# A transformer layer in split fp32: the last output-projection columns by token halves, operand combinations in order of need, and gate2 in 1 KB pieces

## Chip, core and metric

The kernel runs on one core of one Trainium2 chip. The metric is device microseconds of one execution. The median of three runs of the kernel before is 1672.77 us (1672.48 to 1673.21).

## The reference

One layer of a decoder for 1024 tokens of width 1024, all in fp32. What matters here is its end:

```python
mod = c_act @ w_ada[l] + b_ada[l]
shift1, scale1, gate1, shift2, scale2, gate2 = [m[:, None, :] for m in jnp.split(mod, N_MOD, axis=-1)]
...
y = jax.nn.sigmoid(g_a) * y_a + jax.nn.sigmoid(g_b) * y_b
x = layer_norm_affine(ALPHA * x + gate1 * (y @ w_o[l]), ln1_g[l], ln1_b[l])

h2 = layer_norm(x) * (1.0 + scale2) + shift2
u = h2 @ w_up[l]
up = jnp.pad(u, ((0, 0), (CONV_W - 1, 0), (0, 0)))
u = conv_b[l] + sum(conv_w[l, t] * up[:, t:t + S] for t in range(CONV_W))
u_gate, u_val = jnp.split(u, 2, axis=-1)
f = jax.nn.gelu(u_gate, approximate=False) * u_val
x = layer_norm_affine(ALPHA * x + gate2 * (f @ w_down[l]), ln2_g[l], ln2_b[l])
```

`w_o` is 1024 x 1024, `w_up` 1024 x 5632, `w_down` 2816 x 1024, `w_ada` 1024 x 6144.

## The kernel before

**Arithmetic.** Every fp32 operand of TensorE (PE) is split into a high part rounded to fp32r and the rest as a low part, and a product is three matmuls (high by high, high by low, low by high). `split_to()` does it with a cast on ScalarE (ACT, L378) and a subtraction on VectorE (DVE, L379, the tiles ending in `l` or `lo`). The weights come through staging tiles `wst` (four buffers) and `raw` (six).

**Order of the work.** PE's order is written out by hand: `unit()` issues the matmuls of one product, moves a model clock `now` on by a cost, and between them `run_due()` calls whatever `at(delay, ...)` has put into a queue for that moment. The instructions of the other engines follow their place in the program and are set in order from it; every engine, and SyncE (SP), which issues the loads and stores, works off its own list in order.

**Output projection.** `wo_unit(n, t)` computes 256 output columns `n` of token tile `t` (128 tokens): `o_unit()` loads the residual x (tile `th`, later `xt`), runs 24 matmuls into a `pj` bank, and `o_evac()` (L979) adds it to alpha x, giving `y`. The weights are folded with gate1 on their way (L250, cast L252, split L253). Columns 0:256 and 256:512 are done so; the groups of weights are in `g_o`. The last columns, 512:1024, are `o_unit(t, g_o[2], 512, 512, ...)` for the eight token tiles in order, after all 256-column units. At that point the pools of the stage before, with the `th` tiles, are closed, and the pool `hq` takes their place.

**Layer norms.** After each of the last units `ln_a()` takes statistics (L364, L366), gets the reciprocal root `rs` on GpSimd (POOL, L357 and L358), normalises on DVE (L1059, L1060) and stores the row tile; `ln_b()` takes statistics again and writes the second norm on ACT (L1065). `h2_part()` transposes it on PE (L1076), evacuates by ACT (L1081, tiles `xt`, `t3hf`, `t4hf`), and splits: the first 512 tokens on DVE and POOL (L1084, L1085); for the second 512 DVE builds differences.

**Up projection.** It multiplies 2 x 2 blocks of `w_up` and h2 with seven products for eight. The moving operands are the blocks themselves (`h2h`, `h2l`), and the combinations T1 = B12 - B11 (`t3lf` at L1067 first), T2 = B22 - T1 (`t4lf`, then `t2h`/`t2l`), T3 = B22 - B12 (`t3h`/`t3l`) and T4 = B21 - T2 (`t4h`/`t4l`, with L1116). `h2_rest()` writes, after the last part of h2, the splits of T1, then all of T3, then those of B22 and all of T4, each for k = 0 to 3. `product(n)` runs the list `seq`; product 6 uses T2, 7 uses T3, 4 uses T4. Products 4, 6 and 7 share a pair of PSUM banks (`w`); the pair is free again when DVE has added both to the hidden tile `u` (L1244). Weight combinations are summed on POOL (L1179 to L1185), loads are at L1167, the convolution's steps at L1146 (tile `cv`).

**gate2** is a product of a vector and `w_ada`, done on DVE: `ada_part(3, kt)` loads two pieces of 128 x 512 into `wst` buffers (256 KB each, name `aw`), and `ada_acc()` multiplies (L596) or multiplies and adds (L598) them into `gate`. Eight parts follow each other from `ADA3_D = 100` us of the model clock on, every `ADA3_P = 12`; `ada_end(3)` sums over partitions on PE (L615) and adds the bias on DVE (L616).

**The end.** The down projection is accumulated for token tiles in the order `(0, 2, 3, 1)` of each half; `finish()` gates, adds the residual, takes statistics and normalises (L1301 to L1310). For `t == NT - 1` the last step is one DVE operation (L1312), for all others ACT scales (L1314) and POOL adds (L1315).

## Time and profile before

| | |
|---|---|
| median of three runs | 1672.77 us (1672.48 to 1673.21) |
| the profiled execution | 1667.94 us |
| its span, first to last instruction | 1666.2 us |
| mean granted TensorE clock in it | 0.98 |
| busy: PE, DVE, ACT, POOL | 1570.1, 1083.1, 739.0, 509.8 us |
| PE busy from 880 to 980 us | 68.9 of 100 us |

The profiled execution is one run of its own, with its own time; its events are measured from the span's start. "Busy" is the time in which an engine executes an instruction; a wait belongs to the engine's next instruction and is put down to the event that came last (the releaser). The granted clock is given as a share of full speed.

### The profile page before, as it was taken

How to read it: one execution, taken by the hardware profiler on the slowest of the kernel's cores; microseconds unless marked ns; L12 is line 12 of the kernel's file. 1: busy time of each engine (PE TensorE's matmuls, PEld its weight loads, DVE VectorE, ACT ScalarE, POOL GpSimd, SP SyncE). 2: the span in 40 equal slices, each digit the busy share in tenths (PEclk: the TensorE clock that was granted, in tenths of full speed). 3: DMA queues.
4: the chain of work that ended last, by engine and by line, in shares of the span. 5: the costliest groups of instructions: out<-in, count | busy, mean ns of one | idle time of the engine just before them, and what ended most of it. 6: DMA issues, size and time to landing. Idle time of an engine off the chain costs nothing.

```text
span 1666.2 us, 28016 instructions
## 1 busy us (share of the span) xinstructions
PE 1570.1 (94%) x10513; PEld 1389.9 (83%) x10514; DVE 1083.1 (65%) x2092; ACT 739.0 (44%) x1698; POOL 509.8 (31%) x694
## 2 busy tenths in 40 slices
PE   5899999999999999999998768989999999999996
PEld 4899999998998999989996556777788887888885
DVE  7766666675646545535658878777877877437535
ACT  5565555554535544545313624433444444333430
POOL 5523232232633614415316442222332220003103
PEclk9999999999999999999999989999999999999998
DMA  7501000013214032111142322333222215743641
GB/s 248 163 24 36 27 27 27 27 52 116 64 52 127 26 102 89 52 51 29 49 158 95 102 64 76 108 108 104 81 89 82 77 63 197 249 142 115 195 139 51
DMA packets 77769, 153.36 MB, mean 92 GB/s; under 512 B 8753, under 2 KB 11313, under 8 KB 77634
## 3 DMA queue, kind: packets, MB, share of 16 engines
q1 hardware_dynamic: 77634, 151.58, 28.6%
q8 instruction: 82, 1.34, 0.3%
q14 instruction: 53, 0.43, 0.1%
HBM read 131.63 MB, written 19.92 MB: 91 GB/s over the span
## 4 chain that ended last, share of the span: by engine, by line
PE 80%; DVE 9%; DMA 3%; POOL 3%; issue 3%; ACT 2%; SPq 0%; POOLq 0%; ACTq 0%; DVEq 0%
PE pj L334 10%; PE pj L336 10%; PE pj L335 10%; PE w L1292 7%; PE pj L1292 4%; PE m L1292 3%; PE w L1234 3%; PE w L1236 3%; PE w L1235 3%; DMA aw<-in_ada 2%; PE m L712 2%; PE m L1234 2%; PE m L1235 2%; PE m L1236 2%; PE pj L349 2%
## 5 line engine op out<-in xcount | busy, mean ns | idle before, releaser
L334 PE MATMUL pj<-whi,hh 128*128 128x256 f32 (+1 forms) x1296 | 374.0, 289 | 0.1
L336 PE MATMUL pj<-whi,hl 128*128 128x256 f32 (+1 forms) x1296 | 367.7, 284 | 0.0
L335 PE MATMUL pj<-wlo,hh 128*128 128x256 f32 (+1 forms) x1296 | 367.5, 284 | 0.0
L334 PEld LDWEIGHTS pj<-whi,hh 128*128 128x128 f32 x1296 | 248.6, 192 | 0.6 <-issue 0.2
L335 PEld LDWEIGHTS pj<-wlo,hh 128*128 128x128 f32 x1296 | 247.0, 191 | 0.6 <-issue 0.2
L336 PEld LDWEIGHTS pj<-whi,hl 128*128 128x128 f32 x1296 | 246.9, 191 | 0.0
L378 ACT CAST whi<-wst 128x512 fp32r<-128x512 f32 x176 | 107.3, 619 | 152.2 <-PE w L1235 49.2
L379 DVE TENSOR_TENSOR wlo<-wst,whi 128x512 fp32r<-128x512 f32 x176 | 132.2, 762 | 58.7 <-ACT whi L378 58.5
L1146 DVE SCALAR_TENSOR_TENSOR cv<-u,pv_sb,cv 128x1023 f32<-128x1023 f32 x88 | 119.4, 1359 | 12.3 <-ACT cv L1144 12.3
L357 POOL TENSOR_SCALAR rs<-mv 128x1 f32<-128x1 f32 x32 | 15.5, 488 | 319.0 <-DVE mv L1305 249.3
L253 DVE TENSOR_TENSOR wlo<-wst,whi 128x512 fp32r<-128x512 f32 (+1 forms) x108 | 78.5, 744 | 42.1 <-ACT whi L252 41.6
L252 ACT CAST whi<-wst 128x512 fp32r<-128x512 f32 (+1 forms) x116 | 70.5, 620 | 42.7 <-PE pj L336 27.1
L379 DVE TENSOR_TENSOR fl<-wst,fh 128x512 fp32r<-128x512 f32 x41 | 29.0, 708 | 80.6 <-ACT fh L378 80.6
L378 ACT CAST whi<-raw 128x512 fp32r<-128x512 f32 x66 | 40.8, 620 | 90.3 <-PE m L1235 43.3
L691 POOL TENSOR_SCALAR_AFFINE_SELECT pch<-ph 128x512 f16<-128x512 f16 x32 | 20.4, 639 | 195.7 <-ACT ph L686 195.7
L1179 POOL TENSOR_TENSOR raw<-raw 128x512 f32<-128x512 f32 x22 | 33.6, 1528 | 141.2 <-DMA raw<-in_wup 69.1
L1185 POOL TENSOR_TENSOR wst<-wst 128x512 f32<-128x512 f32 x22 | 35.8, 1626 | 127.6 <-issue 88.3
L1234 PE MATMUL pj<-h2h,whi 128*128 128x512 f32 x176 | 70.6, 401 | 1.7 <-ACT u L1241 1.7
L1236 PE MATMUL pj<-h2h,wlo 128*128 128x512 f32 x176 | 69.8, 397 | 1.5 <-DVE wlo L379 1.5
L1235 PE MATMUL pj<-h2l,whi 128*128 128x512 f32 x176 | 69.8, 396 | 0.0
L1234 PE MATMUL m<-h2h,whi 128*128 128x512 f32 x176 | 69.8, 396 | 0.0
L1235 PE MATMUL m<-h2l,whi 128*128 128x512 f32 x176 | 69.2, 393 | 0.0
(441 smaller groups left out, 4469.9 us busy)
## 6 DMA issues: line engine op xcount, KB each, us to landing
wst<-in_wbig SPq DMA_DIRECT2D x112, 256.0 KB, 3.1
aw<-in_ada SPq DMA_DIRECT2D x96, 256.0 KB, 3.2
wst<-in_wdn SPq DMA_DIRECT2D x88, 256.0 KB, 3.1
wst<-in_wup SPq DMA_DIRECT2D x52, 256.0 KB, 2.6
raw<-in_wup SPq DMA_DIRECT2D x44, 256.0 KB, 3.4
fd<-cv SPq DMA_DIRECT2D x22, 512.0 KB, 4.1
wst<-fd SPq DMA_DIRECT2D x44, 256.0 KB, 3.1
y<-in_x SPq DMA_DIRECT2D x8, 512.0 KB, 8.4
```

The source lines that it names most:

```text
L252: act.copy(out=hi, in_=st)
L253: lo_eng.tensor_tensor(out=lo, in0=st, in1=hi.bitcast(F32), op=ALU.subtract)
L334: pe.matmul(acc, lhsT=lh, rhs=wh, start=kt == 0 if start is None else start, stop=False)
L335: pe.matmul(acc, lhsT=lh, rhs=wl, start=False, stop=False)
L336: pe.matmul(acc, lhsT=ll, rhs=wh, start=False, stop=kt == NK - 1 if stop is None else stop)
L378: act.copy(out=hl[0], in_=src)
L379: dve.tensor_tensor(out=hl[1], in0=src, in1=hl[0].bitcast(F32), op=ALU.subtract)
L1146: dve.scalar_tensor_tensor(out=c_[:, lag:S], in0=u[:, 0:S - lag], scalar=wv[:, 2 - lag:3 - lag], in1=c_[:, lag:S], op0=ALU.mult, op1=ALU.add)
L1234: pe.matmul(acc, lhsT=wh[:, kt, :], rhs=bh, start=p not in (2, 3) and kt == 0, stop=False, **go)
L1235: pe.matmul(acc, lhsT=wh[:, kt, :], rhs=bl, start=False, stop=False, **go)
L1236: pe.matmul(acc, lhsT=wl[:, kt, :], rhs=bh, start=False, stop=kt == 3, **go)
L1292: pe.matmul(acc, lhsT=l_[:, ts_], rhs=r_, start=i == 0 and n == 0, stop=i == NFF - 1 and n == 2)
```

## The change

1. The last columns' weights are no longer streamed by `ws`. Eight pieces are loaded to `wst`, multiplied by the gate, and split into the slots of T3 and T4 (`t_slot(3, ...)`, `t_slot(4, ...)`), which are free until the second half of h2.
2. The eight last-columns units and the four units of columns 256:512 of the second token half are one list: the first last-columns unit comes first, then they alternate.
3. `h2_rest()` is gone. `t1_t3(k)` and `b22_t4(k)` are put into the queue one by one, every 2.0 and 2.6 us of the model clock.
4. gate2 is computed by 32 pieces of 128 x 256 (1 KB per partition) and four of one row for the bias, in one buffer of its own (`aw3`), from 70 us of the model clock on, one every 8.5. ACT evacuates the sums of `ada3_end()`.
5. In `finish()` the one-operation DVE path is taken for the last tile worked on in the second half.


```diff
--- before.py
+++ after.py
@@ -34,8 +34,9 @@
 B_FIRST = 3
 B_LAST = (3, 5)
 MOD_PE = 1
-ADA3_D = 100.0
-ADA3_P = 12.0
+ADA3_D = 70.0
+ADA3_P = 8.5
+T3_P, T4_P = 2.0, 2.6
 ADA_D = 5.0
 ADA_E = 8
 LN_D = 5.0
@@ -285,11 +286,14 @@
         g_qk.append(add_group())
         g_ga.append(add_group())
         g_v.append(add_group())
-    g_o = [add_group(fold=(0, slice(0, 256))), add_group(fold=(0, slice(256, 512))),
-           add_group(fold=(0, slice(512, 1024)), shape=(1, 512), n=8)]
+    g_o = [add_group(fold=(0, slice(0, 256))), add_group(fold=(0, slice(256, 512)))]
+    wi_o2 = wi
+
     def kslice(ids, kt):
 
         base = 0
+        if isinstance(ids[0], tuple):
+            return ids[kt]
         for w_ in ids:
             n = ws.items[w_][1][0]
             if kt < base + n:
@@ -1028,7 +1032,7 @@
     yT[1] = new_yT(1)
     for t in range(4):
         at((0.3, 2.0, 4.0, 9.5)[t], 0.87, lambda t=t: y_transpose(4 + t))
-    for n, t in ((1, 0), (1, 1), (0, 4), (1, 2), (0, 5), (1, 3), (0, 6), (1, 4), (0, 7)):
+    for n, t in ((1, 0), (1, 1), (1, 2), (1, 3), (0, 4), (0, 5), (0, 6), (0, 7)):
         wo_unit(n, t)
     assert not queue
     s2ctx.close()
@@ -1044,11 +1048,16 @@
         return hq.tile([P, 512], dtype, name=f"t{m}{hl}" + ("" if dtype == F32R else "f"), tag=f"t{m}{hl}", bufs=4)
 
     g1b, b1b = (hq.tile([P, D], F32, name=n_, tag="t2h", bufs=2) for n_ in ("g1b", "b1b"))
-    for t in range(5, NT):
-        wo_unit(1, t)
-    sp.dma_start(g1b, rows[2])
-    sp.dma_start(b1b, rows[3])
-    ws.get(g_o[2][-1])
+    g_o2 = []
+    for kt in range(NK):
+        st = wp.tile([P, 512], F32, name="wst", tag="wst", bufs=4)
+        sp.dma_start(st, wbig[wi_o2 + kt])
+        if kt == 3:
+            sp.dma_start(g1b, rows[2])
+            sp.dma_start(b1b, rows[3])
+        dve.tensor_tensor(out=st, in0=st, in1=gate[:, 512:1024], op=ALU.mult)
+        g_o2.append(tuple(t_slot(3 + kt // 4, hl, kt % 4) for hl in "hl"))
+        split_to(g_o2[kt], st)
     h2 = [None, None]
 
     def ln_a(t):
@@ -1097,40 +1106,65 @@
             tt_[2][k] = t2h[0][:, k % 2, :], t_slot(2, "l", k)
             split_to(tt_[2][k], t2)
 
-    def h2_rest():
-
-        for k in range(4):
-            split_to([hl[:, :, k, :] for hl in h2[1]], rows4(tmp.pop(("t1", k))))
-        for k in range(4):
-            b12, b22 = tmp.pop(("b", k)), tmp["b", 4 + k]
-            t3 = hq.tile([P, 512], F32, name="xt", tag="raw", bufs=6)
-            sub(t3, b22, b12)
-            tt_[3][k] = [t_slot(3, hl, k) for hl in "hl"]
-            split_to(tt_[3][k], t3)
-        for k in range(4):
-            b22 = rows4(tmp.pop(("b", 4 + k)))
-            split_to([hl[:, :, 4 + k, :] for hl in h2[1]], b22)
-            t4 = hq.tile([P, 512], F32, name="xt", tag="raw", bufs=6)
-            b21 = [hl[:, :, 4 + k, :].bitcast(F32) for hl in h2[0]]
-            sub(rows4(t4), b21[0], rows4(tmp.pop(("t2", k))))
-            dve.tensor_tensor(out=rows4(t4), in0=rows4(t4), in1=b21[1], op=ALU.add)
-            tt_[4][k] = [t_slot(4, hl, k) for hl in "hl"]
-            split_to(tt_[4][k], t4)
+    def t1_t3(k):
+
+        b12, b22 = tmp.pop(("b", k)), tmp["b", 4 + k]
+        t3 = hq.tile([P, 512], F32, name="xt", tag="raw", bufs=6)
+        sub(t3, b22, b12)
+        tt_[3][k] = [t_slot(3, "h", k), None]
+        act.copy(out=tt_[3][k][0], in_=t3)
+        split_to([hl[:, :, k, :] for hl in h2[1]], rows4(tmp.pop(("t1", k))))
+        tt_[3][k][1] = t_slot(3, "l", k)
+        dve.tensor_tensor(out=tt_[3][k][1], in0=t3, in1=tt_[3][k][0].bitcast(F32), op=ALU.subtract)
+
+    def b22_t4(k):
+
+        b22 = rows4(tmp.pop(("b", 4 + k)))
+        split_to([hl[:, :, 4 + k, :] for hl in h2[1]], b22)
+        t4 = hq.tile([P, 512], F32, name="xt", tag="raw", bufs=6)
+        b21 = [hl[:, :, 4 + k, :].bitcast(F32) for hl in h2[0]]
+        sub(rows4(t4), b21[0], rows4(tmp.pop(("t2", k))))
+        dve.tensor_tensor(out=rows4(t4), in0=rows4(t4), in1=b21[1], op=ALU.add)
+        tt_[4][k] = [t_slot(4, hl, k) for hl in "hl"]
+        split_to(tt_[4][k], t4)
 
     def ln_tile(t):
         ln_a(t)
         at(LN_D, 0.0, lambda: ln_b(t))
 
-    for t in range(NT):
-        o_unit(t, g_o[2], 512, 512, lambda: ln_tile(t))
-        if t % 4 == 3:
-            for n in range(NK):
-                kt = n if t == 3 else n // 2 + 4 * (n % 2)
-                at(H2_D + H2_P * n, 0.45, lambda kt=kt, t=t: h2_part(t // 4, kt))
-    at(H2_D + H2_P * NK, 0.0, h2_rest)
-    for kt in range(NK):
-        at(ADA3_D + ADA3_P * kt, 0.0, lambda kt=kt: ada_part(3, kt))
-    at(ADA3_D + ADA3_P * NK + 40.0, 1.7, lambda: ada_end(3))
+    def ada3_part(kt, j):
+
+        cs = slice(256 * j, 256 * j + 256)
+        aw = hq.tile([P, 256], F32, name="aw3")
+        if kt < NK:
+            sp.dma_start(aw, ada2[3 * NK + kt][:, cs])
+            ada_acc(aw, cs, kt)
+        else:
+            sp.dma_start(aw[0:1, :], rows[1][0:1, cs])
+            dve.tensor_tensor(out=gate[0:1, cs], in0=gate[0:1, cs], in1=aw[0:1, :], op=ALU.add)
+
+    def ada3_end(i):
+        cs = slice(512 * i, 512 * i + 512)
+        pt = ps1("m")
+        pe.matmul(pt, lhsT=ones, rhs=gate[:, cs], start=True, stop=True)
+        act.copy(out=gate[:, cs], in_=pt)
+
+    for n, t in ((2, 0), (1, 4), (2, 1), (1, 5), (2, 2), (1, 6), (2, 3), (1, 7), (2, 4), (2, 5), (2, 6), (2, 7)):
+        if n < 2:
+            wo_unit(n, t)
+        else:
+            o_unit(t, g_o2, 512, 512, lambda: ln_tile(t))
+        if n == 2 and t % 4 == 3:
+            for m in range(NK):
+                kt = m if t == 3 else m // 2 + 4 * (m % 2)
+                at(H2_D + H2_P * m, 0.45, lambda kt=kt, t=t: h2_part(t // 4, kt))
+    for k in range(4):
+        at(H2_D + H2_P * NK + T3_P * k, 0.0, lambda k=k: t1_t3(k))
+        at(H2_D + H2_P * NK + T3_P * 4 + T4_P * k, 0.0, lambda k=k: b22_t4(k))
+    for m in range(4 * (NK + 1)):
+        at(ADA3_D + ADA3_P * m, 0.0, lambda m=m: ada3_part(m // 4, m % 4))
+    for i in range(2):
+        at(ADA3_D + ADA3_P * 4 * (NK + 1) + 10.0 * i, 1.4, lambda i=i: ada3_end(i))
 
 
 
@@ -1291,7 +1325,7 @@
         for n, (l_, r_) in enumerate(((fh, wh), (fh, wl), (fl, wh))):
             pe.matmul(acc, lhsT=l_[:, ts_], rhs=r_, start=i == 0 and n == 0, stop=i == NFF - 1 and n == 2)
 
-    def finish(s, tl):
+    def finish(s, tl, last):
         t = 4 * s + tl
         z = xts.pop(t)
         st = sq.tile([P, 2, 6], F32, name="bst")
@@ -1308,7 +1342,7 @@
             cs = slice(512 * hf, 512 * hf + 512)
             zs = z[:, cs]
             dve.scalar_tensor_tensor(out=zs, in0=zs, scalar=mv[:, 0:1], in1=g2b[:, cs], op0=ALU.subtract, op1=ALU.mult)
-            if t == NT - 1:
+            if last:
                 dve.scalar_tensor_tensor(out=zs, in0=zs, scalar=rs, in1=b2b[:, cs], op0=ALU.mult, op1=ALU.add)
             else:
                 act.activation(out=zs, in_=zs, func=AF.Identity, scale=rs)
@@ -1358,7 +1392,7 @@
             for hf in range(2):
                 for i in range(NFF - n_last, NFF):
                     down_mm(s, i, tl, hf)
-            finish(s, tl)
+            finish(s, tl, s == 1 and tl == order[-1])
```

The planned order of three lists shows what moved. First DVE's list at the first last-columns evacuation (`y<-xt,pj 128x512`) and its weight splits. Before:
```order
L253 TENSOR_TENSOR wlo<-wst,whi 128x512
L250 TENSOR_TENSOR wst<-wst,gate 128x512 x3
L979 SCALAR_TENSOR_TENSOR y<-xt,pj 128x256 x2
L253 TENSOR_TENSOR wlo<-wst,whi 128x512 x3
L979 SCALAR_TENSOR_TENSOR y<-xt,pj 128x256
L250 TENSOR_TENSOR wst<-wst,gate 128x512
L253 TENSOR_TENSOR wlo<-wst,whi 128x512
L979 SCALAR_TENSOR_TENSOR y<-xt,pj 128x512
L364 BN_STATS bst<-y 128x6
L366 BN_AGGR mv<-bst 128x2
L1059 SCALAR_TENSOR_TENSOR y<-y,mv,g1b 128x1024
```
After the change:
```order
L983 SCALAR_TENSOR_TENSOR y<-th,pj 128x256 x6
L383 TENSOR_TENSOR t3l<-wst,t3h 128x512 x4
L1058 TENSOR_TENSOR wst<-wst,gate 128x512 x2
L383 TENSOR_TENSOR t4l<-wst,t4h 128x512
L1058 TENSOR_TENSOR wst<-wst,gate 128x512
L383 TENSOR_TENSOR t4l<-wst,t4h 128x512
L1058 TENSOR_TENSOR wst<-wst,gate 128x512
L383 TENSOR_TENSOR t4l<-wst,t4h 128x512 x2
L983 SCALAR_TENSOR_TENSOR y<-xt,pj 128x512
L368 BN_STATS bst<-y 128x6
L370 BN_AGGR mv<-bst 128x2
L1068 SCALAR_TENSOR_TENSOR y<-y,mv,g1b 128x1024
```
The four `t3l` splits and four `t4l` splits of the last weights stand where the stream's `wlo` splits stood; the evacuation of the 512-column unit comes before four of the 256-column ones instead of behind them.

Then DVE's list around the first evacuation of a product into `u`. Before:
```order
L1067 TENSOR_TENSOR xt<-h2h,t4lf 128x512
L379 TENSOR_TENSOR h2l<-t4hf,h2h 128x4x128
L379 TENSOR_TENSOR t4l<-xt,t4h 128x512
L1116 TENSOR_TENSOR xt<-xt,h2l 128x512
L1067 TENSOR_TENSOR xt<-h2h,t4lf 128x512
L379 TENSOR_TENSOR wlo<-raw,whi 128x512
L379 TENSOR_TENSOR t4l<-xt,t4h 128x512
L1116 TENSOR_TENSOR xt<-xt,h2l 128x512
L1244 TENSOR_TENSOR u<-w_13674,u 128x512
L379 TENSOR_TENSOR wlo<-wst,whi 128x512
L379 TENSOR_TENSOR t4l<-xt,t4h 128x512
L1244 TENSOR_TENSOR u<-w_13674,u 128x512
```
After the change:
```order
L383 TENSOR_TENSOR t2l<-t4lf,t2h 128x512
L1118 TENSOR_TENSOR t3l<-xt,t3h 128x512
L383 TENSOR_TENSOR h2l<-t3lf,h2h 128x4x128
L383 TENSOR_TENSOR wlo<-raw,whi 128x512
L1118 TENSOR_TENSOR t3l<-xt,t3h 128x512
L1076 TENSOR_TENSOR xt<-t4hf,t3hf 128x512
L383 TENSOR_TENSOR h2l<-t3lf,h2h 128x4x128
L1278 TENSOR_TENSOR u<-w_13622,u 128x512
L1118 TENSOR_TENSOR t3l<-xt,t3h 128x512
L383 TENSOR_TENSOR wlo<-wst,whi 128x512
L1076 TENSOR_TENSOR xt<-t4hf,t3hf 128x512
L383 TENSOR_TENSOR h2l<-t3lf,h2h 128x4x128
```
The evacuation stood behind all T3 and nearly all T4 work; it now stands ahead of half of the T3 splits and of all T4 work.

Last, SP's list of loads and stores in the part where the last token tiles are normalised. Before:
```order
L987 DMA xt<-in_x 128x512
L1061 DMA x1d<-y 128x1024 x6
L987 DMA xt<-in_x 128x512
L1167 DMA wst<-in_wup 128x512
L1061 DMA x1d<-y 128x1024
L1167 DMA raw<-in_wup 128x512 x2
L1167 DMA wst<-in_wup 128x512 x2
L1167 DMA raw<-in_wup 128x512 x2
L1167 DMA wst<-in_wup 128x512
L1061 DMA x1d<-y 128x1024
```
After the change (`aw_...` are the loads of gate2):
```order
L991 DMA xt<-in_x 128x512
L1070 DMA x1d<-y 128x1024
L1140 DMA aw_14161<-in_ada 128x256
L1140 DMA aw_14230<-in_ada 128x256
L1070 DMA x1d<-y 128x1024
L1140 DMA aw_14301<-in_ada 128x256
L1140 DMA aw_14366<-in_ada 128x256
L1201 DMA wst<-in_wup 128x512 x2
L1070 DMA x1d<-y 128x1024
L1201 DMA wst<-in_wup 128x512 x2
L1140 DMA aw_14426<-in_ada 128x256
L1070 DMA x1d<-y 128x1024
```
The loads of gate2, which came behind this part, now stand between the weight loads and the stores of the normalised rows.

## Rows read from the trace of the kernel before

**Rows 1.** The page, part 1: busy time of each engine, its share, instructions.
```profile
PE 1570.1 (94%) x10513; PEld 1389.9 (83%) x10514; DVE 1083.1 (65%) x2092; ACT 739.0 (44%) x1698; POOL 509.8 (31%) x694
```

**Rows 2.** Busy time by stretches: stretch, length, engines, PEclk (granted clock), DMA share, GB/s.
```profile
880.00:980.00 100.00, 68.92 (x306) 53.64 (x305) 82.13 (x123) 45.56 (x71) 54.13 (x55) 0.90 0.27 87
...
960.00:980.00 20.00, 10.01 (x37) 8.07 (x38) 15.55 (x23) 3.82 (x7) 13.21 (x7) 0.67 0.20 54
```

**Rows 3.** PE's waits, 860 to 1000: who <- for whom: total us, times, longest.
```profile
PE w L1234 <- DVE u L1244: 14.5, 2, 13.7
```

**Rows 4.** DVE's time line: start, us, instruction, [idle before <- releaser].
```profile
863.53 0.69 DVE L979 SCALAR_TENSOR_TENSOR y<-xt,pj 128x512 f32<-128x512 f32 x1 [1.78 <-PE pj L336]
...
934.66 1.78 DVE L1067 TENSOR_TENSOR t3lf<-t3hf,h2h 128x512 f32<-128x512 f32 x1
...
954.80 0.68 DVE L379 TENSOR_TENSOR t2l<-t4lf,t2h 128x512 fp32r<-128x512 f32 x1
...
956.00 1.89 DVE L1067 TENSOR_TENSOR xt<-t4hf,t3hf 128x512 f32<-128x512 f32 x3
...
969.24 0.69 DVE L1244 TENSOR_TENSOR u<-w,u 128x512 f32<-128x512 f32 x1
```

**Rows 5.** PE's waits, 1000 to 1320.
```profile
PE w L1234 <- DVE u L1244: 17.5, 5, 5.9
PE m L615 <- DVE gate L616: 0.8, 1, 0.8
```

**Rows 6.** PE's time line in the gate2 stretch.
```profile
1067.82 0.51 PE L1234 MATMUL w<-t4h,whi 128*128 128x512 f32 x1 [0.77 <-DVE u L1244]
...
1087.83 0.79 PE L1234 MATMUL w<-t3h,whi 128*128 128x512 f32 x1 [5.86 <-DVE u L1244]
...
1092.93 0.40 PE L1234 MATMUL m<-h2h,whi 128*128 128x512 f32 x1
...
1132.40 0.50 PE L1234 MATMUL w<-t3h,whi 128*128 128x512 f32 x1 [3.19 <-DVE u L1244]
...
1175.02 0.50 PE L1234 MATMUL w<-t3h,whi 128*128 128x512 f32 x1 [2.03 <-DVE u L1244]
```

**Rows 7.** DVE's time line at the eighth unit of the projection.
```profile
846.35 0.42 DVE L979 SCALAR_TENSOR_TENSOR y<-th,pj 128x256 f32<-128x256 f32 x1 [2.45 <-PE pj L336]
847.71 2.12 DVE L253 TENSOR_TENSOR wlo<-wst,whi 128x512 fp32r<-128x512 f32 x3 [0.94 <-ACT whi L252]
...
851.29 1.32 DVE L250 TENSOR_TENSOR wst<-wst,gate 128x512 f32<-128x512 f32 x2 [0.52 <-DMA wst<-in_wbig]
```

**Rows 8.** The tile gate, 1000 to 1250: instructions (min/median/max ns), DVE's idle before them.
```profile
L598 DVE SCALAR_TENSOR_TENSOR gate<-aw,csil,gate x14: 740/752/1344, 1068.9 to 1163.5; 128x512 f32<-128x512 f32 x14
...
  DMA aw<-in_ada: 14.9, 12
```

**Rows 9.** DMA issues: count, size, median us to landing (from 810; from 1040).
```profile
th<-in_x SPq DMA_DIRECT2D x10, 128.0 KB, 2.2
...
aw<-in_ada SPq DMA_DIRECT2D x16, 256.0 KB, 3.1
```

**Rows 10.** DVE's time line at the first pair of gate2 pieces.
```profile
1048.60 0.49 DVE L596 TENSOR_SCALAR gate<-aw,csil 128x512 f32<-128x512 f32 x1 [1.06 <-DMA aw<-in_ada]
...
1052.48 0.49 DVE L596 TENSOR_SCALAR gate<-aw,csil 128x512 f32<-128x512 f32 x1 [2.20 <-DMA aw<-in_ada]
```

**Rows 11.** Time lines of DVE, ACT and POOL at the end.
```profile
1653.56 1.41 DVE L1312 SCALAR_TENSOR_TENSOR xr<-xr,rs,b2b 128x512 f32<-128x512 f32 x2
...
1659.77 1.33 ACT L1314 ACTIVATE xr<-xr,rs 128x512 f32<-128x512 f32 x2 [13.12 <-POOL rs L358]
...
1660.56 2.48 POOL L1315 TENSOR_TENSOR xr<-xr,b2b 128x512 f32<-128x512 f32 x2 [0.83 <-ACT xr L1314]
```

**Rows 12.** DVE by line, 862 to 975: busy us, mean ns | idle before.
```profile
L1060 DVE SCALAR_TENSOR_TENSOR y<-y,rs,b1b 128x1024 f32<-128x1024 f32 x8 | 12.3, 1537 | 4.8 <-POOL rs L358 4.6
```

**Rows 13.** Waits of SP's own queue, 840 to 1000.
```profile
SPq L1167 <- DVE wlo L379: 70.7, 18, 27.1
```

## The prediction, made before the changed kernel ran

> **What bounds the kernel now.** I read the page first: TensorE (PE) is busy for 94% of the span [rows 1], so a change pays only where PE stands. The busy time by stretches shows where that is: between 880 and 980 us PE loses 31 of 100 us. In the last 20 of them it works 10.0 us while VectorE (DVE) works 15.6, and the granted clock has fallen to 0.67 of full speed, between its two levels of 1.2 and 2.4 GHz [rows 2]. The table of PE's waits names the largest of these losses: 13.7 us for the DVE evacuation of `u` at L1244 [rows 3]. DVE's own time line shows why. The chain begins at 863.5, when the first last-columns product is evacuated; the first T1 difference (`t3lf`) comes at 934.7, the last low part of T2 at 954.8, and the `u` evacuation for which PE waits only at 969.2, because h2_rest() put nearly all T1, T3, `b22` and T4 work ahead of it [rows 4]. So DVE bounds the stretch 863 to 970, and PE has products ready to run that wait for one 0.6 us evacuation behind 14 us of operands for later products. A second place is the accumulation of gate2 (1045 to 1210): PE waits for `u` there again, at 1067.8, 1087.8, 1132.4 and 1175.0; with one of 5.6 us before it, at 1006, these are the five of the table [rows 5, 6].
>
> A difference of 0.2% (3.3 us) is about what a measurement of this kernel can tell from none.
>
> **The change, term by term.** The sum is made against the profiled execution, 1667.9 us (span 1666.2); the median of the runs shown is 4.8 us above that.
>
> *Start of the last columns.* Four 256-column units move behind the first 512-column one. Units follow each other by 2.85 us, so that product could begin at 846.4, when the eighth unit is evacuated [rows 7], instead of 857.8 (its 24 matmuls at 0.24 us take 5.7, and its evacuation starts at 863.5): 11.4 us earlier. But its weights now lie in `t3`/`t4` slots of a pool that takes over the memory of the `th` tiles, and the eighth unit reads the last `th`; in the order on DVE the four `t3l` splits stand behind that evacuation. So the splits run when they ran before, from about 847.5 [rows 7]; only then are the four staging buffers reloaded. The reloaded pieces reach their multiplication at 851.3 [rows 7], as before; multiply, cast and split take some 0.6 us each, and four pieces leave a split every 1.1 us, so the last is ready at 856.6 and the product is evacuated at 857.3. PE stands about 5 us at 848 to 856 in pieces under 2.5 us. **Gain at this point 6.2 us**, not 11.4.
>
> *DVE up to the first T1 difference.* Counted in DVE's order with steps from the trace (0.6 us for a 128x512 operation: three in 1.89 [rows 4]; 1.22 for two of them; 0.4 for 256 columns), the rows from that evacuation to `t3lf` add up to 54.8 us before and 63.6 after: twelve gate2 pieces (4.8), four 256-column evacuations (1.6) and three weight splits (1.8) have been put among them, with half a microsecond of statistics. Before, the stretch took 71.1 us [rows 4], so 16.3 of it were waits and stretched instructions. I keep 12.5 of those: the waits for the reciprocal root on POOL are now partly filled by the added evacuations. `t3lf` is then at 857.3 + 63.6 + 12.5 = 933.4, **only 1.3 us earlier** than before: the early start is spent on the added work.
>
> *Order of need.* Between `t3lf` and the first `u` evacuation DVE has 18.5 us of rows after the change, and took 34.6 before. The T2 low parts were not done before 20.8 us (954.8 + 0.7 - 934.7 [rows 4]); this included a pause of some 5 us in which ACT waited, so it is the outer bound, and 18.5 the inner. I take 20, nearer the outer one: ACT and DVE still hand tiles to each other. The evacuation comes at 953.4 instead of 969.2, 15.9 us earlier with the 1.3. Behind it PE has five more products of 2.9 us before the first T4 product; the last T4 part on DVE ends some 19 us after the evacuation, PE would want it at 18, so I charge 1.5 us. **Net 14.4 us.** What is late next is DVE itself: its T4 work ends near 973. The gain is PE work run beside it.
>
> *gate2.* Before, 16 pieces of 512 columns cost DVE 0.75 us each (the first two 0.49) plus 14.9 us of waits for their DMA [rows 8, 10]. PE paid 11.9 us of waits for `u` (0.77 + 5.86 + 3.19 + 2.03 [rows 6]) and 0.8 for the final evacuation [rows 5]. It also paid for the clock: the group at 1087.83 took 5.1 us to 1092.93 instead of 2.8 [rows 6], after an idle of 5.9 us, on the lower of the two levels; I put 1.5 us on the wait of 3.2 at 1132. Together 16.4. After, 36 pieces of 256 columns (four of one row) go through one buffer: load k+1 is issued only when piece k has been added. A load of 128 KB lands 2.2 us after its issue, one of 256 KB after 3.1 [rows 9]. Fourteen pieces now sit before the T4 work; the other 22 start near 985. In the order, two or three pieces of each 20 us period stand one or two 0.6 us rows behind the previous one, so DVE waits 1 to 1.6 us each time; with 5 x 0.4 of work that is 4.6 to 5.6 us per period. How much DVE can lose before PE notices is shown by the first pair: 1.06 + 2.20 of waiting and 2 x 0.49 of work [rows 10] gave a PE wait of 0.77 [rows 6], so 3.5 us are free. That leaves 1.1 to 2.1 us in each of five periods, 8 us with the clock, and 1.5 in the first wave, which already has a wait of 5.6. **Gain 16.4 - 9.5 = 7 us** (bounds: -10, rival 2, and +14).
>
> The Trainium skill, page "DMA: Bandwidth & Descriptors", section "Anatomy of one DMA — SWDGE (gpsimd) path", has a DMA of that path cost about 2.0 us however small, plus bytes at 436 GB/s (these loads are SP's): by that rule a piece of 128 KB costs 2.3 us against 2.6, and halving the pieces nearly doubles the waiting of a single-buffered chain. The trace agrees on the small transfer (2.2) and shows more for the large one (3.1), and the chain that this would make is rival 2.
>
> *The tail.* The last token tile is t=5 (order 0, 2, 3, 1), but before it was t=7 that took the short DVE path. Now t=5 does. The two operations of t=7 (1.41 us, from 1653.56 [rows 11]) leave DVE's path, and the last tile needs 1.4 us on DVE instead of ACT from 1659.77 and POOL until 1660.56 + 2.48 = 1663.04 [rows 11]. POOL's two additions for t=7 now stand before the last root, to about 1656.8; root 1.7, then 1.4 on DVE: 1659.95. **Gain 3 us.**
>
> The diff's delays and constants only place these rows; I price them at nothing beyond the above. Sum: 14.4 + 7 + 3 = 24.4, so 1643.5 for the profiled execution, **1648 us** against the median.
>
> **Rivals.**
> 1. *The gain shrinks to about 10 us.* The twelve early pieces each keep DVE waiting 1.2 us, the mean of before (14.9 / 12 [rows 8]): 14.4 us in the stretch that DVE bounds. Or POOL does it: eight of its raw-weight sums, not two, now stand before the last tile's root. For it: in-order queues. Against: most early pieces have 3 us of other rows between them, and the wait for the last tile's transposes covers three of them. 1672.8 - 10 = 1663. The Trainium skill, page "SBUF — State Buffer", section "Who interferes with whom", says that a DVE instruction with two SBUF inputs contends with a POOL instruction that reads SBUF. The trace shows DVE's normalisation step at a mean of 1537 ns [rows 12], with the stretched ones beside such POOL work; this would push the same way.
> 2. *Slower.* The gate2 loads stand in SP's queue behind weight loads and stores that wait for DVE: 70.7 us of SP waits in 18 places before [rows 13]. If a piece is issued late, DVE stands at it, the weight slots come free later, and the queue holds the next one. At a full 2.2 us for each piece, the twelve early ones cost another 22 us and the late ones turn +7 into -10: 14.4 + 3 - 22 - 10 = -15, so 1688. It decides from about 1.3 us of waiting per piece. Against: the piece is issued as soon as its predecessor is added wherever SP's head is free.
> 3. *It doesn't do what it says.* The last weights come so late that `t3lf` moves to 940 and T2's operands with it, the slower clock stays, and the gates eat the rest: 1672.
> 4. *More than forecast*: no wait of PE at all from 1000 on, the one at 1006 included: 14.4 + 3 + 16.4 + 5.6 = 39.4, so 1633.
>
> **How the numbers follow.** Forecast (1639 to 1657) 0.55; rival 1 (1657 to 1668) 0.20; rival 2 0.11; rival 3 0.08; rival 4 0.06. The range 1638 to 1668 leaves out rivals 2, 4 and part of 3, two in ten. Faster by over 0.2%: 0.81; within: 0.08; slower: 0.11.
>
> **What would show it.** Right: the 13.7 us wait of PE gone, with the first two T2 products under 6 us apart; the first 512-column evacuation at 856 to 858; `t3lf` at 931 to 937; waits for `u` between 1000 and 1210 adding to under 12 us; no ACT or POOL on the last output. Wrong: `t3lf` after 940, DVE waits for `aw` in 860 to 940 above 10 us, or SP waits that end just before an `aw` load.

## The result and the profile after

The changed kernel takes 1652.95 us (median of four runs, 1650.26 to 1653.32) against 1672.62 in the same measurement: a ratio of 0.988, 95% interval 0.9863 to 0.9897, 19.7 us faster. The forecast was 1648, within 1638 to 1668. The total came out near the forecast; its terms did not, and this section and the runs are about that. One run of the last version below took 2548.61 us, at a granted clock of 0.56, and stands in no median here.

The page, part 1, answers to [rows 1]:

```profile
PE 1578.2 (96%) x10514; PEld 1392.8 (84%) x10514; DVE 1097.4 (66%) x2110; ACT 740.3 (45%) x1700; POOL 512.8 (31%) x694
```

The busy time by stretches, as in [rows 2]:

```profile
880.00:980.00 100.00, 85.22 (x383) 67.41 (x382) 88.55 (x133) 42.63 (x65) 50.65 (x53) 0.91 0.28 92
960.00:980.00 20.00, 14.91 (x49) 11.16 (x50) 20.00 (x29) 8.07 (x15) 7.11 (x4) 0.83 0.13 35
```

PE is busy for 85.2 of the 100 us instead of 68.9. That looks like 16 us won here, and is not: 45 of the 96 matmuls of the four moved units and 23 more of the last columns now lie in the stretch, which both kernels pass at much the same mean granted clock (0.90 before, 0.91 now). DVE is now busy for all 20 us of the last part.

**A mark to count from.** PE's list is the same in both kernels until long after the wait for `yTl`. That wait ends at 822.86 us in the profiled execution of before and at 826.99 in this one, so 4.1 us of lateness were there before the change could act. All places below are counted from this mark; spans counted from it are 1666.2 - 822.86 = 843.3 and 1651.5 - 826.99 = 824.5, a gain of 18.8 us. PE's time line of before, then of the changed kernel: the mark, a wait that both have in the third wave of products, and the last matmul.

```profile
822.86 1.09 PE L833 MATMUL w<-ident,y 128*128 128x128 f32 x8 [1.51 <-DVE yTl L837]
...
1006.26 0.77 PE L1234 MATMUL w<-t3h,whi 128*128 128x512 f32 x1 [5.63 <-DVE u L1244]
...
1652.85 0.39 PE L1292 MATMUL m<-whi,fl 128*128 128x512 f32 x1
```

```profile
826.99 1.09 PE L837 MATMUL w<-ident,y 128*128 128x128 f32 x8 [1.82 <-DVE yTl L841]
...
965.48 0.79 PE L1268 MATMUL w<-t2h,whi 128*128 128x512 f32 x1 [3.48 <-DVE u L1278]
...
986.79 0.50 PE L1268 MATMUL w<-t4h,whi 128*128 128x512 f32 x1 [1.22 <-ACT t4h L382]
...
989.44 0.79 PE L1269 MATMUL w<-t4l,whi 128*128 128x512 f32 x1 [2.15 <-DVE t4l L383]
...
1007.87 0.50 PE L1268 MATMUL w<-t3h,whi 128*128 128x512 f32 x1 [3.21 <-DVE u L1278]
...
1084.69 0.50 PE L1268 MATMUL w<-t3h,whi 128*128 128x512 f32 x1 [1.80 <-DVE u L1278]
...
1640.87 0.39 PE L1326 MATMUL m<-whi,fl 128*128 128x512 f32 x1
```

At the wait in the third wave (`w<-t3h`) PE stands at 183.4 us after the mark before and at 180.9 now: **only 2.5 us** have been won by then. At the last matmul it stands at 830.0 and 813.9: 16.1 us, so **13.6 us** came between, in the stretch of gate2. What lies behind the last matmul is 13.35 us before (1666.2 - 1652.85) and 10.63 now: **2.7 us** from the end.

PE's waits from 860 to 1000 and from 1000 to 1340, as in [rows 3, 5]:

```profile
PE w L1268 <- DVE u L1278: 5.1, 3, 3.5
PE pj L1268 <- ACT u L1275: 4.2, 2, 2.7
PE m L1085 <- ACT xt L1090: 3.9, 1, 3.9
PE w L1269 <- DVE t4l L383: 2.1, 1, 2.1
```

```profile
PE w L1268 <- DVE u L1278: 6.1, 5, 3.2
```

The wait of 13.7 is gone. In its place stand the first of 3.5, a set of waits for T4 (1.22 and 2.15 above), and 3.21 in the third wave. Behind 1010 the five waits of before (11.9 for `u`, 0.8 for the end of gate2) have shrunk to 0.17, 0.36, 1.80 and 0.59.

DVE's time line, as in [rows 4]: the first and last of the eight last-columns evacuations, the first T1 difference, the first `u`, the last part of T4.

```profile
862.71 0.69 DVE L983 SCALAR_TENSOR_TENSOR y<-xt,pj 128x512 f32<-128x512 f32 x1 [1.62 <-PE pj L340]
...
927.16 0.67 DVE L983 SCALAR_TENSOR_TENSOR y<-xt,pj 128x512 f32<-128x512 f32 x1
...
946.34 0.69 DVE L1076 TENSOR_TENSOR t3lf<-t3hf,h2h 128x512 f32<-128x512 f32 x1
...
964.75 0.68 DVE L1278 TENSOR_TENSOR u<-w,u 128x512 f32<-128x512 f32 x1
...
987.63 1.75 DVE L383 TENSOR_TENSOR t4l<-xt,t4h 128x512 fp32r<-128x512 f32 x1
```

The same for the last of the eight evacuations of before:

```profile
915.38 0.62 DVE L979 SCALAR_TENSOR_TENSOR y<-xt,pj 128x512 f32<-128x512 f32 x1
```

From the mark: the first evacuation is 5.0 us earlier than before (35.7 against 40.7), the last 7.7 us later (100.2 against 92.5), the first T1 difference 7.5 later (119.35 against 111.8), the first `u` 8.6 earlier (137.8 against 146.4), the last part of T4 12.6 later (160.6 against 148.1).

The tile gate, as in [rows 8]: pieces, and DVE's idle before them.

```profile
L602 DVE SCALAR_TENSOR_TENSOR gate<-aw,csil,gate x28: 461/486/1521, 888.9 to 1092.3; 128x256 f32<-128x256 f32 x28
...
  DMA aw<-in_ada: 7.4, 10
```

The end, as in [rows 11], on POOL and DVE:

```profile
1642.26 2.93 POOL L1349 TENSOR_TENSOR xr<-xr,b2b 128x512 f32<-128x512 f32 x2 [0.83 <-ACT xr L1348]
1645.20 0.78 POOL L361 TENSOR_SCALAR rs<-mv 128x1 f32<-128x1 f32 x1
1646.06 0.93 POOL L362 TENSOR_TENSOR rs<-rs,mhalf 128x1 f32<-128x1 f32 x1
```

```profile
1647.02 1.42 DVE L1346 SCALAR_TENSOR_TENSOR xr<-xr,rs,b2b 128x512 f32<-128x512 f32 x2 [0.46 <-POOL rs L362]
```

### The profile page after: what moved, and what is told of

It is laid out like the page before. It is cut to its first block, busy times and chain, and to the rows that moved or that the text cites. A ratio compares the mean times of both kernels' runs of the same rounds, so it can differ in the third digit from the quotient of the medians.

```text
span 1651.5 us, 28042 instructions
## 1 busy us (share of the span) xinstructions
PE 1578.2 (96%) x10514; PEld 1392.8 (84%) x10514; DVE 1097.4 (66%) x2110; ACT 740.3 (45%) x1700; POOL 512.8 (31%) x694
## 4 chain that ended last, share of the span: by engine, by line
PE 78%; DVE 10%; DMA 3%; POOL 3%; ACT 2%; issue 2%; SPq 1%; POOLq 0%; DVEq 0%; ACTq 0%
PE pj L338 10%; PE pj L339 10%; PE pj L340 10%; PE w L1326 7%; PE pj L1326 4%; PE m L1326 3%; PE w L1268 3%; PE w L1270 3%; PE w L1269 3%; DVE cv L1180 2%; PE m L716 2%; PE pj L353 2%; PE m L755 2%; PE pj L354 2%; PE pj L355 2%
## 5 line engine op out<-in xcount | busy, mean ns | idle before, releaser
L361 POOL TENSOR_SCALAR rs<-mv 128x1 f32<-128x1 f32 x32 | 16.1, 502 | 318.1 <-DVE mv L1339 244.9
L254 DVE TENSOR_TENSOR wlo<-wst,whi 128x512 fp32r<-128x512 f32 (+1 forms) x100 | 72.7, 745 | 40.4 <-ACT whi L253 39.2
L253 ACT CAST whi<-wst 128x512 fp32r<-128x512 f32 (+1 forms) x108 | 65.5, 620 | 19.2 <-PE pj L354 10.9
```

Source lines behind the costliest of these rows:

```text
L253: act.copy(out=hi, in_=st)
L254: lo_eng.tensor_tensor(out=lo, in0=st, in1=hi.bitcast(F32), op=ALU.subtract)
```

## The experiments

Theory 1, made from the profile above: DVE bounds everything up to the last T4 part, and the fourteen gate2 pieces that now lie there are what delays the first T1 difference. (They take 7.8 us by their rows; twelve of them, 6.8 us, stand ahead of that difference.)

### First four: one part undone, alone, or late

`gate_undone` puts the old gate2 back into the changed kernel:

```diff
...
-    for m in range(4 * (NK + 1)):
-        at(ADA3_D + ADA3_P * m, 0.0, lambda m=m: ada3_part(m // 4, m % 4))
...
+    for kt in range(NK):
+        at(ADA3_D + ADA3_P * kt, 0.0, lambda kt=kt: ada_part(3, kt))
+    at(ADA3_D + ADA3_P * NK + 40.0, 1.7, lambda: ada_end(3))
```

> The change with gate2 as before (16 pieces of 512 columns through the staging buffers, after the T4 work). Theory 1: up to the last T4 part DVE is the bound, and the fourteen early pieces (6.7 us of DVE work and their waits) sit in it; without them the first T1 difference comes about 8 us earlier and some 6 us of that reach the end, while the 13.7 us that gate2 saved behind 1006 are lost: about 1661. Rival: the early pieces only fill time in which DVE waits anyway; then nothing comes back and the whole 13.7 are lost: about 1667.

1669.41 us, ratio 0.9984 (0.9973 to 0.9995).

`gate_alone` is the reverse, the kernel before with `ada3_part()` and `ada3_end()` of the change added:

```diff
-        at(ADA3_D + ADA3_P * kt, 0.0, lambda kt=kt: ada_part(3, kt))
...
+        at(ADA3_D + ADA3_P * m, 0.0, lambda m=m: ada3_part(m // 4, m % 4))
...
```

> The kernel before with gate2 by 256-column pieces in a buffer of its own, and nothing else. Theory 1: 13.7 us won behind 1006, 6 to 8 lost ahead of it, where DVE bounds: about 1666. Rival (early pieces free): 13.7 won, about 1659.

1659.27 us, ratio 0.9922 (0.9907 to 0.9937).

`gate_late` makes every piece read factors that are handed over by the last T4 part:

```diff
+        if k == 3:
+            dve.scalar_tensor_tensor(out=csil_l, in0=tt_[4][k][1][:, 0:NK].bitcast(F32), scalar=0.0, in1=csil,
+                                     op0=ALU.mult, op1=ALU.add)
...
```

> The change, but all 36 pieces made to wait for the last T4 part (one tiny DVE operation hands the factors over there). Theory 1: the stretch up to the T4 work gets shorter by about 6 us, the later pieces give back 1 to 2: about 1649. Rival (early pieces free): nothing is won there, and 14 more pieces stand in the later stretch: 1653 to 1657.

1660.50 us, ratio 0.9924 (0.9907 to 0.9941).

`comb_undone` is the change with h2_rest() again:

```diff
...
-    for k in range(4):
-        at(H2_D + H2_P * NK + T3_P * k, 0.0, lambda k=k: t1_t3(k))
-        at(H2_D + H2_P * NK + T3_P * 4 + T4_P * k, 0.0, lambda k=k: b22_t4(k))
+    at(H2_D + H2_P * NK, 0.0, h2_rest)
```

> The change with the T1, T3, B22 and T4 work in the order of before (all T3 first, then all T4). Theory 1: DVE has the same sum of work up to the last T4 part, so the order of need is worth 3 us or less at 1006: about 1656. The prediction's term: it is worth 14 us, so about 1667.

1655.26 us, ratio 0.99 (0.9886 to 0.9915).

**Theory 1 fell on the pieces, inside the change**: with none of them in front (`gate_late`, `gate_undone`) the first T1 difference came no earlier (121.7 and 122.0 after the mark, against 119.35 in the change), and making them late cost 7.5 us. Beside the old output projection the pieces do delay it (116.4 in `gate_alone`, 111.8 before), but the first `u` came no later there (145.5 against 146.4): the start of T1 alone decides little. The theory held on the order of need, which by the medians is worth 2.3 us inside the change and not 14; the intervals of the two overlap, and from the mark PE ends 1.8 us later without it. In `comb_undone` PE's big wait is back, in its waits from 880 to 990, and 2.3 us are all that reaches the end:

```profile
PE w L1264 <- DVE u L1274: 15.3, 2, 14.9
```

That left the output projection as the cause to try for the late T1. Theory 2: the last weights in the T3/T4 slots hold up the chain to the last unit.

### Second four: the output projection, and what helps gate2

`halves_undone` keeps all else of the change, but units and weights of the output projection are those of before:

```diff
-            o_unit(t, g_o2, 512, 512, lambda: ln_tile(t))
...
+    for t in range(5, NT):
+        wo_unit(1, t)
...
+    ws.get(g_o[2][-1])
...
+        o_unit(t, g_o[2], 512, 512, lambda: ln_tile(t))
```

> The change with the units and the streamed weights of the output projection as before; combinations in order of need, gate2 in pieces and the end as changed. Theory 2: the 5 us for which TensorE stands at the start of the last columns, because their weights wait for the slots, are put on the chain to the last unit, whose evacuation comes 7.7 us later than before, and with it everything that needs the second half of the tokens; undone, the first T1 difference comes some 3 us and the first evacuation into u some 3 us earlier than in the change: about 1650. Rival: the parts add (undoing the order of need cost 2.3 us, the change is 3.6 us ahead of gate2 alone with the end), so the halves are worth about 1 us: 1654 to 1655.

**1648.25 us**, ratio 0.9853 (0.9835 to 0.987): faster than the change.

`halves_cover` and `halves_last` keep the slots and change the order of the units:

```diff
-    for n, t in ((2, 0), (1, 4), (2, 1), (1, 5), (2, 2), (1, 6), (2, 3), (1, 7), (2, 4), (2, 5), (2, 6), (2, 7)):
+    for n, t in ((1, 4), (1, 5), (2, 0), (1, 6), (2, 1), (1, 7), (2, 2), (2, 3), (2, 4), (2, 5), (2, 6), (2, 7)):
...
+    for n, t in ((1, 4), (1, 5), (1, 6), (1, 7), (2, 0), (2, 1), (2, 2), (2, 3), (2, 4), (2, 5), (2, 6), (2, 7)):
```

> The change with two of the four 256-column units ahead of the first last-columns unit, so that the weights are split while TensorE works on those. Theory 2: the 5 us of waits at the start are covered, the last unit and the first T1 difference come up to 5 us earlier than in the change: 1648 to 1650. Rival: DVE bounds from there to the T4 work whatever TensorE does, so nothing is won: 1653.

1651.81 us, ratio 0.9876 (0.9861 to 0.9891), between the two expectations. PE still stood 4.75 us at the start, for the evacuation of a bank, and the last unit came at 99.9 after the mark.

> The change with all four 256-column units ahead of the last-columns units, as in the kernel before, but with the weights still in the T3 and T4 slots. Theory 2: no wait at the start, the last unit as early as before or earlier: as the version without halves, 1649 to 1651, and if the two are alike, the loss is the wait for the slots and not the slots themselves. Rival: 1653 to 1655.

1657.66 us, ratio 0.9909 (0.9894 to 0.9924): a miss. The wait at the start was not covered. DVE's time line of `halves_last` shows the splits standing ahead of the evacuation of a unit long done:

```profile
855.05 2.50 DVE L383 TENSOR_TENSOR t3l<-wst,t3h 128x512 fp32r<-128x512 f32 x4 [0.73 <-ACT t3h L382]
858.53 1.34 DVE L1058 TENSOR_TENSOR wst<-wst,gate 128x512 f32<-128x512 f32 x2 [0.99 <-DMA wst<-in_wbig]
...
863.43 0.41 DVE L983 SCALAR_TENSOR_TENSOR y<-xt,pj 128x256 f32<-128x256 f32 x1
```

and PE's time line shows it waiting for that evacuation's bank:

```profile
863.90 0.58 PE L338 MATMUL pj<-whi,yTh 128*128 128x256 f32 x1 [4.36 <-DVE y L983]
```

`gate_staging` takes the small pieces' buffers from the weights' staging tiles:

```diff
-        aw = hq.tile([P, 256], F32, name="aw3")
+        aw = wp.tile([P, 512], F32, name="aw3", tag="wst", bufs=4)[:, 0:256]
```

> The change with gate2 by the same 36 small pieces, but in the four staging buffers of the weights instead of a buffer of its own; they then come behind the T4 work, as where all pieces are late (1660.5). Theory 2: what gate2 cost before is that its pieces hold the buffers in which the next weights should arrive; so, with twice as many slots taken, 1668 to 1675. Rival: the size of the pieces is what counts; then as with late pieces in their own buffer, 1659 to 1662.

1663.63 us, ratio 0.9945 (0.9929 to 0.9962): outside both expected ranges, nearer to the rival's. From the mark PE ends at 824.0 here and at 824.4 in `gate_late`, where all pieces are late too; with the old pieces (`gate_undone`) at 831.7. So with all pieces late the small ones are worth 7.5 us. They are also spread over more time (1033 to 1301 us here, 988 to 1160 in `gate_late`, 1051 to 1167 in `gate_undone`), and no run tells size from spacing. What the buffer is worth at equal lateness stays open: the profiles show nothing, the medians 3.1 us for the buffer of its own, and the two intervals overlap. DVE's idle for gate2 loads is larger in the staging buffers. The tile gate in `gate_late`, then in `gate_staging`:

```profile
  DMA aw<-in_ada: 12.9, 17
```

```profile
  DMA aw<-in_ada: 35.4, 20
```

The buffer of its own pays in another way: it lets fourteen pieces come before T4. That is the step from `gate_late` to the change, 7.5 us by the medians.

### Last four

`halves_mixed` has the first four of the last weights in the stream's tiles and four in the T4 slots:

```diff
-        g_o2.append(tuple(t_slot(3 + kt // 4, hl, kt % 4) for hl in "hl"))
+        g_o2.append(tuple(t_slot(4, hl, kt % 4) for hl in "hl") if kt > 3 else
+                    tuple(wp.tile([P, 512], F32R, name=n_, tag=n_) for n_ in ("whi", "wlo")))
```

> The change with the first four of the last weights in the stream's own tiles and only the last four in the T4 slots. Theory 2: what costs is that splits which wait for the slots stand ahead of evacuations in DVE's list; with half of them the first last-columns evacuation comes 3 to 5 us earlier than in the change and the last unit 2 to 4 us earlier: 1649 to 1651. Rival: the order by token halves itself costs, and the slots do not: 1653.

1653.09 us, ratio 0.9891 (0.9875 to 0.9907). The first evacuation came at 34.8 after the mark and the last at 102.5: theory 2's remedy did not work. It had not taken the wait away either. PE stood 3.6 us in the first last-columns unit (3.9 in the change), most of it at one T4 slot, and its granted clock from 20 to 40 us after the mark was 0.83 (0.91 in the change, 1.00 before):

```profile
858.71 0.80 PE L338 MATMUL pj<-t4h,yTh 128*128 128x512 f32 x1 [2.42 <-ACT t4h L382]
```

`order_alone` is the kernel before with the edit of `comb_undone` the other way round, and nothing else.

> The kernel before with the T1, T3, B22 and T4 work in order of need, and nothing else. Theory 2: without the slots in front of it the order of need brings the first evacuation into u some 11 us earlier and, as DVE stays the bound up to T4, 6 to 8 us of the time: 1665 to 1667. The prediction's term (14 us, with the start): 1658. Rival: it needs the gate2 pieces gone from the staging buffers to show: 1670 or more.

1667.23 us, ratio 0.9977 (0.9967 to 0.9986), 4.1 us under the 1671.30 of before on that chip. Its PE time line:

```profile
827.60 1.09 PE L834 MATMUL w<-ident,y 128*128 128x128 f32 x8 [1.61 <-DVE yTl L838]
...
964.45 0.80 PE L1239 MATMUL w<-t2h,whi 128*128 128x512 f32 x1 [3.35 <-DVE u L1249]
...
987.32 0.68 PE L1240 MATMUL w<-t4l,whi 128*128 128x512 f32 x1 [2.15 <-DVE t4l L380]
989.21 0.80 PE L1239 MATMUL w<-t4h,whi 128*128 128x512 f32 x1 [0.78 <-DVE u L1249]
...
1008.47 0.79 PE L1239 MATMUL w<-t3h,whi 128*128 128x512 f32 x1 [5.55 <-DVE u L1249]
```

The second T2 product starts 136.9 us after the mark instead of 147.1, 10.3 earlier; at `w<-t3h` it is 180.9 instead of 183.4. So 10 us are won and nearly 8 given back within 45 us, as waits for T4 and as matmuls of 0.63 us at the lower clock behind them.

`change_again` is the changed kernel once more, and `halves_undone_again` the version with the old output projection, on one chip.

> The change once more, beside the version without slots: 1653 by every theory.

1652.31 us, ratio 0.9884 (0.9867 to 0.9902).

> The version with units and weights of the output projection as before, once more beside the change: by theory 2 about 5 us less than the change, 1648; if the parts merely add, 1653 to 1655.

**1646.78 us** (median of four runs, 1644.72 to 1650.12), ratio 0.9853 (0.9834 to 0.9872). The version without the new output projection was 5.5 us faster on this chip and 4.7 in the earlier measurements. The intervals of the two just overlap each time, but its eight runs lie between 1644.7 and 1651.1 (mean 1647.6), the nine of the change between 1649.2 and 1653.8 (mean 1652.0). It is the fastest version run. Its DVE time line, last unit, T1, `u`, T4:

```profile
919.40 0.63 DVE L982 SCALAR_TENSOR_TENSOR y<-xt,pj 128x512 f32<-128x512 f32 x1
...
943.95 0.68 DVE L1070 TENSOR_TENSOR t3lf<-t3hf,h2h 128x512 f32<-128x512 f32 x1
...
961.60 0.68 DVE L1269 TENSOR_TENSOR u<-w,u 128x512 f32<-128x512 f32 x1
...
984.50 1.74 DVE L382 TENSOR_TENSOR t4l<-xt,t4h 128x512 fp32r<-128x512 f32 x1
```

Eight of the profiles side by side, us after each one's own mark (827.32 in the last), and what lies behind PE's last matmul:

| | first, last unit | first T1 | first `u` | last T4 | PE's last | behind it |
|---|---|---|---|---|---|---|
| before | 40.7, 92.5 | 111.8 | 146.4 | 148.1 | 830.0 | 13.35 |
| the change | 35.7, 100.2 | 119.4 | 137.8 | 160.6 | 813.9 | 10.63 |
| gate_undone | 36.3, 99.9 | 122.0 | 139.5 | 161.8 | 831.7 | 10.65 |
| gate_alone | 40.6, 92.0 | 116.4 | 145.5 | 147.2 | 816.5 | 13.21 |
| order_alone | 40.5, 92.5 | 111.9 | 136.1 | 157.9 | 825.9 | 13.34 |
| halves_last | 46.4, 100.3 | 122.6 | 140.6 | 163.5 | 816.0 | 10.57 |
| halves_mixed | 34.8, 102.5 | 120.2 | 137.8 | 160.8 | 814.4 | 10.53 |
| halves_undone_again | 40.7, 92.1 | 116.6 | 134.3 | 157.2 | 810.5 | 10.59 |

Every version with weights in the slots has its last unit at 98.7 to 102.5, in three orders of the units; every one with streamed weights at 92.0 to 92.5.

## Why the prediction was right in the sum and wrong in its terms

**Start of the last columns: nearly right as a row, wrong as a gain.** The first evacuation came 5.0 us earlier (6.2 forecast; 858.6 on the clock of before, just outside the 856 to 858 that the prediction named), for the reason given: splits that wait for the slots. The failing step is "Gain at this point 6.2 us". Four units of 2.85 us, 11.4 in all, now lie between the first and the last of the eight. Coming 5.0 earlier instead of 11.4 is a loss of 6.4 for whatever needs the last unit, and T1 needs it. The last unit came 7.7 us later, and the text had the 5 us of standing PE in the same paragraph. The profiles have 3.9 us of it, and a granted clock of 0.91 from 20 to 40 us after the mark and of 0.83 from 80 to 100, where before had 1.00 in both.

**DVE up to T1: wrong.** Forecast 933.4; measured 946.3, or 942.2 on the clock of before (4.1 less). The step counted DVE rows (63.6) and kept 12.5 us of waits; the stretch took 946.34 - 862.71 = 83.6. Busy time of PE, PEld, DVE, ACT and POOL in it, before and then after:

```profile
863.53:934.66 71.13, 60.21 (x279) 47.54 (x277) 58.44 (x88) 23.14 (x30) 43.18 (x54) 1.00 0.35 120
```

```profile
862.71:946.34 83.63, 74.15 (x362) 60.72 (x361) 70.97 (x107) 25.29 (x34) 49.00 (x56) 0.94 0.42 139
```

DVE was idle for 12.7 us both times, so the waits came out right, and its rows took 71.0, 7.4 us more than counted. But its rows alone do not set the time: in `gate_late`, without the pieces, DVE is busy for 65.1 us of the same stretch, which takes 86.1. PE has 14 us more work here than before, the moved units among it, and T1 follows the last unit by 19.2 us, 19.3 before. So the reading is that T1 is late because the last unit is. It is not proof: in the other versions T1 follows by 17.7 to 24.5.

**Order of need: mis-sized, 14.4 forecast, 2.5 measured** with the start, 4.1 alone. From T1 to `u` the order did what was forecast (18.4 us; 18.5 to 20). Two things failed. T1 itself was 8.8 us later than forecast. And "the last T4 part on DVE ends some 19 us after the evacuation" was 24.6 (from 964.75 to 989.38), with PE standing at T4 and again at 1007.9: a reordering on an engine that stays busy moves the wait. `order_alone` shows it without the other parts.

Most of that excess of some 5 us has rows. DVE's time line behind the first `u`, and POOL's beside it:

```profile
965.35 1.16 DVE L1118 TENSOR_TENSOR t3l<-xt,t3h 128x512 fp32r<-128x512 f32 x1
966.43 1.76 DVE L383 TENSOR_TENSOR wlo<-wst,whi 128x512 fp32r<-128x512 f32 x1
968.11 1.79 DVE L1076 TENSOR_TENSOR xt<-t4hf,t3hf 128x512 f32<-128x512 f32 x1
969.82 1.77 DVE L383 TENSOR_TENSOR h2l<-t3lf,h2h 128x512 fp32r<-128x512 f32 x1
971.52 0.68 DVE L383 TENSOR_TENSOR h2l<-t4hf,h2h 128x512 fp32r<-128x512 f32 x1
```

```profile
966.03 1.61 POOL L1214 TENSOR_TENSOR raw<-wst,raw 128x512 f32<-128x512 f32 x1
967.72 1.63 POOL L1215 TENSOR_TENSOR wst<-raw,wst 128x512 f32<-128x512 f32 x1
969.43 1.61 POOL L1219 TENSOR_TENSOR wst<-wst 128x512 f32<-128x512 f32 x1
```

Operations of 0.68 us take 1.76 to 1.79 while POOL sums raw weights, and 0.68 again once it has ended; with the 1.16 here and the 1.75 of the last T4 part they come to 4.8 us more than five of 0.68. It is not always DVE that is held up: at 984.30 a sum of POOL takes 2.86 us beside DVE operations of 0.68. The Trainium skill, page "SBUF — State Buffer", section "Who interferes with whom", says that a DVE instruction with two SBUF inputs contends with a POOL instruction that reads SBUF; these rows agree. The sum had only 0.6 us steps for this stretch.

**gate2: mis-sized the other way, 7 forecast, 13.6 measured** (13.4 alone, by the medians). The forecast left 9.5 us of loss; PE's waits for `u` behind 1010 add to 2.9, and the clock from 1060 to 1100 is 1.00 where it was 0.91. DVE waited 7.4 us for ten of the 32 loads, not 1 to 1.6 for two or three pieces in each period. The 3.5 us that DVE may lose unnoticed were read from one pair of pieces, and they count ahead of one evacuation, not, as the step had it, over a period of 20 us. Two of the three pieces that stood ahead of the evacuation for which PE waited 5.86 us before, and the first of two ahead of PE's longest wait behind 1010 now:

```profile
1074.68 1.34 DVE L598 SCALAR_TENSOR_TENSOR gate<-aw,csil,gate 128x512 f32<-128x512 f32 x1 [3.10 <-DMA aw<-in_ada]
...
1078.77 0.75 DVE L598 SCALAR_TENSOR_TENSOR gate<-aw,csil,gate 128x512 f32<-128x512 f32 x1 [1.54 <-DMA aw<-in_ada]
```

```profile
1074.77 1.33 DVE L602 SCALAR_TENSOR_TENSOR gate<-aw,csil,gate 128x256 f32<-128x256 f32 x1 [1.63 <-DMA aw<-in_ada]
```

With the third piece (0.74) the set of before took 7.5 us, so 1.6 were free there and not 3.5; the set of now took 4.4 with its second piece, and PE waited 1.80. Before, sets of two or three pieces fell ahead of one evacuation; now it is one or two. `gate_staging`, with 35.4 us of DVE waits and PE ending as in `gate_late` with 12.9, shows that the sum of the waits is not what counts.

The Trainium skill, page "DMA: Bandwidth & Descriptors", section "Anatomy of one DMA — SWDGE (gpsimd) path", has about 2.0 us as the fixed cost of a load that GpSimd issues, and the bytes at 436 GB/s on top. The prediction's estimate from that page was 2.3 us for a load of 128 KB and 2.6 for one of 256. These loads are SP's, and their medians from issue to landing were 2.5 now and 3.1 before, so half the bytes did cost most of the time. The chain of waits that the prediction made of it as its rival 2 did not appear.

**The tail: right**, 2.7 against 3.

**The rivals.** Rival 1 (early pieces keep DVE waiting) did not happen: DVE waited for two of the fourteen. Rival 2 neither. Rival 3's mechanism did: T1 behind 940, T2 with it, the slower clock. It cost the front of the change nearly all its gain, and gate2 covered it. So the two big errors, 12 us too much and 6.6 too little, partly cancelled: that the total lay near the forecast was luck. Of the signs that the prediction named, the gone wait, the waits for `u` behind 1000 (6.1 us) and the end came as said; the first T1 difference lay behind 940, which it had named as a sign of being wrong, and the first two T2 products were 7.9 us apart (957.57 to 965.48), not under 6.

**Open.** The parts do not add: order of need alone 4.1, gate2 alone 13.4 and the end 2.7 make 20.2, but together, without the slots, they gave 24.5 and 24.6. The profiles place the surplus ahead of the wait in the third wave: with both, PE stands there at 177.7 after the mark (`halves_undone_again`), against 183.4 before, 180.9 with the order alone and 184.4 with gate2 alone. PE's wait of 5.4 us for `t4hf` behind T1, which before and `order_alone` have, is at most 0.8 in `gate_alone` and `halves_undone_again`, which have the early pieces; no run shows why. And what makes the last unit late with weights in the slots is not separated: the waits at the start and the lower clock behind them stand in every such version, in `halves_mixed` too, and without the pieces (`gate_undone`, `gate_late`) it comes at 99.9 and 99.6. Token halves with all weights streamed would tell, and were not tried: the stream's eight pairs of tiles do not hold the twelve that this needs.

## What to carry to other kernels

A unit that starts earlier because others were moved behind it has won nothing until the last of its kind ends earlier: follow the chain from the one that is needed last. Reordering for need pays only as far as the busy engine's sum of work up to the next shared point allows; look there for the waits that come back. When an off-path engine's small jobs make the bound engine wait, make them small, spread them to one an evacuation and give them a buffer that lets them come early; the runs show these together and do not price them one by one.

## What was not expected of the hardware

The mark, ahead of anything the change touches, lay anywhere from 822.9 to 830.4 us in fourteen profiled executions; two of the changed kernel itself had it at 827.0 and 824.6. What moves it was not looked for. Differences of a few microseconds between two profiles mean nothing until they are counted from a place that both share.
